# Neighbourhood attention with two heads on the array's halves, and routing tables stored in the layout of the tile

## The chip, the cores and the metric

One core of one Trainium2 chip runs the whole program. The time of a run is the device time of one execution in microseconds (us); lower is better. The kernel before took 2160.51 us (median of three runs, 2156.67 to 2163.53).

## The reference

Two transformer blocks in sequence over 512 tokens of width 1024. The first has a gated delta rule and a dilated window attention. The second mixes the tokens in three ways (4 heads of HGRN, 4 of RWKV7, 8 of neighbourhood attention over a grid of 8 rows by 64 columns), projects the mix with `w_out`, and ends in a mixture of experts (32 experts, two per token). The change is in the neighbourhood attention and in the tables of the router:

```python
def one_row(r):                       # all 8 rows share one window here
    s_win = einsum('bhjqd,bhrjkd->bhjqrk', q_row, k_blk) * scale     # 8 x 32 keys near a block of 16 columns
    s_win = where(in_win, s_win + rpb[...], NEG_INF)
    s_ctx = einsum('bhjqd,bhld->bhjql', q_row, kc_h) * scale         # 256 context keys, no bias
    prob  = softmax(concatenate([s_win, s_ctx], -1))
    return einsum(p_win, v_blk) + einsum(p_ctx, vc_h)
```

So each of 8 heads has four column blocks j; a head and block has 128 queries (8 rows x 16 columns), 256 window keys, 256 context keys, and head size 64.

## The kernel before, in words

The kernel is written in tiles; a scheduler places each engine's instructions by priority and by readiness, and an engine then runs its list in order. What stands where on an engine is therefore a result of the whole program.

**Neighbourhood attention** is the generator `na()` (kept in `self.heads`; one `next` issues one unit). A pair p of heads (p = 0 to 3) lies on the 128 partitions of q and k, head b on half b of them. `prepare(p)` loads and rotates q and k and loads the values `nvw` (window) and `nvt` (context) and the bias `nb`. There are 32 units (p, j, b):
- `scores`: two matmuls of 64 rows by 256 columns (L1630 window, L1631 context) into one PSUM bank `ns`; on DVE the bias and the maximum (L1633), the maximum of the context half (L1635) and the negated larger one (L1636); on ACT two exponentials of 256 columns that also sum (L1637, L1638).
- `turned`: four 128x128 transposes (L1644) into the bank `nT` and a copy to SBUF, by DVE for b = 1 (L1647), by ACT for b = 0 (L1649).
- `values`: four matmuls (L1658) with the turned probabilities as the stationary 128x128 operand and 64 value columns moving, into a quarter of the bank `no`. After the eighth of a pair the result is divided by the sums (L1663 to L1666) and `put_one` turns it back (L1678) and splits it into the high and low parts `mxh` and `mxl` (L1681, L1682).

**Around it.** The first unit is prepared at the start of `hgrn()` and `na_beside` issues one unit between the steps of HGRN; all others follow in the loop of `run()`, which at unit `na_at` also issues `out_start()` and the output projection of k = 0 and 1. The output projection of k multiplies one 128-row slice of the mix, as high and low parts, by `w_out`: for each of 8 column blocks m three fp32r matmuls of 512 columns (L312 to L314, `mm3`) per k into a PSUM bank `g` (three banks in the pool `gp`), then one DVE instruction that adds the block to x (L1789). The weights `wo` come through SP's DMA queue, ACT makes the high part (L297), POOL the low (L298). k = 4 to 7 use the four pairs of the attention. Then come `tail`, `route` and `experts`.

**The tables.** `route` stores the index and weight tables of the lots beyond the first 32 into DRAM (`ovi`, L2032; `ovw`, L2035), from tiles with the slot on the partition to tables with the lot first, so an element of 8 or 4 bytes at a time. SP issues these stores and then `eod` and the expert weights `er` (1 MB each, L2101). Only the loop of `more_experts` reads the tables, and it runs no times on these inputs.

Of the kernel before, what the change touches and what calls it, by code (L numbers as in the profile page):

```python
# [10 lines left out]
F32 = mybir.dt.float32  # L11
# [7 lines left out]
P = 128  # L19
# [175 lines left out]
def na_bias(rpb):  # L195

    q, k = np.arange(P), np.arange(256)
# [8 lines left out]
    return np.ascontiguousarray(np.stack(out, 2))  # L206
# [64 lines left out]
class Kern:  # L271
# [1282 lines left out]
    def na(self):  # L1554
# [20 lines left out]
        def prepare(p):  # L1575
# [31 lines left out]
            bias = nw.tile([P, 2, 3, 256], F32, tag="nb", name=self.name("nb"), bufs=2)  # L1607
            nc.sync.dma_start(bias, I["b_na"][2 * p:2 * p + 2].rearrange("b p k x -> p b k x"))
# [9 lines left out]
        def scores(p, j, b):  # L1618

            nonlocal ready  # L1620
            if j + b == 0:
                work[p] = (*ready, nw.tile([P, 4, 2, 3], F32, tag="nst", name=self.name("nst"), bufs=2))
                if p < 3:
                    ready = prepare(p + 1)
            q, k, vt, vw, bias, st = work[p]
            r, s = half[b], lambda i: st[:, j, b, i:i + 1]
# [5 lines left out]
            pr = nw.tile([P, T], F32, tag="np", name=self.name("np"), bufs=4)  # L1632
            nc.vector.tensor_tensor_reduce(out=pr[:, :256], in0=ps[:, :256], in1=bias[:, b, (0, 1, 1, 2)[j], :],  # L1633
                                           scale=1.0, scalar=NEG, op0=OP.add, op1=OP.max, accum_out=s(0))
            nc.vector.tensor_reduce(s(1), ps[:, 256:], AX.X, OP.max)  # L1635
            nc.vector.tensor_scalar(s(2), s(0), s(1), -1.0, OP.max, OP.mult)  # L1636
            nc.scalar.activation(pr[:, :256], pr[:, :256], AF.Exp, bias=s(2), accum_out=s(0))  # L1637
            nc.scalar.activation(pr[:, 256:], ps[:, 256:], AF.Exp, bias=s(2), accum_out=s(1))  # L1638
            return pr

        def turned(b, pr):
            pt = psum("nT", self.nt)
            for x in range(4):
                nc.tensor.transpose(pt[:, x * P:(x + 1) * P], pr[:, x * P:(x + 1) * P], ident)  # L1644
            pT = nw.tile([P, T], F32, tag="nT", name=self.name("npT"), bufs=3)
            if b:
                nc.vector.tensor_copy(pT, pt)  # L1647
            else:
                nc.scalar.activation(pT, pt, AF.Copy)  # L1649
            return pT  # L1650

        def values(p, j, b, pT):
            q, k, vt, vw, bias, st = work[p]
            if j + b == 0:
                self.po = psum("no", 1).rearrange("p (j b d) -> p j b d", j=4, b=2)
            hv = half[b]
            for x, v in enumerate((vw[:, j, 0, hv], vw[:, j, 1, hv], vt[:, 0, hv], vt[:, 1, hv])):
                nc.tensor.matmul(self.po[:, j, b, :], pT[:, x * P:(x + 1) * P], v, start=x == 0, stop=x == 3)  # L1658
            if (j, b) != (3, 1):
                return  # L1660

            den = nw.tile([P, 4, 2], F32, tag="nden", name=self.name("nden"), bufs=2)
            nc.vector.tensor_add(den, st[:, :, :, 0], st[:, :, :, 1])  # L1663
            nc.vector.reciprocal(den, den)
            on = nw.tile([P, 4, P], F32, tag="no", name=self.name("non"), bufs=2)
# [665 lines left out]
```

## Time and profile before

| | before |
|---|---|
| device time, median of three runs | 2160.51 us (2156.67 to 2163.53) |
| the profiled execution: time | 2169.63 us |
| the profiled execution: span | 2167.8 us |
| busy: PE, weight loads, DVE, ACT, POOL | 88%, 63%, 45%, 31%, 27% |
| mean granted TensorE clock | 0.882 |

The profile is of one execution, 9.1 us longer than the median of the runs. The engines are PE (matmul), PEld (weight load), DVE, ACT, POOL and SP, which issues most DMAs; the granted clock (PEclk) is a share of 2.4 GHz, so that 0.50 is 1.2 GHz. The shares above are means over stages that are bound by different things; the rows below are therefore taken from the stages that the change touches. An fp32 matmul leaves two records in the trace, an fp32r matmul or a transpose one.

### The profile page before, as it was taken

Reading aid. Unit: us, or ns where it says so; the run is one execution under the profiler, and the core shown is the slowest. Engines: PE = TensorE matmul, PEld = TensorE weight load, DVE = VectorE, ACT = ScalarE, POOL = GpSimd, SP = SyncE. Lnnn points to the kernel's source line nnn. Section 1 sums busy time; section 2 is a strip of 40 time slices with the busy share of each in tenths; the row PEclk is TensorE's granted clock in tenths of the full one; section 3 lists DMA queues with packets and bytes.
Section 4 is the critical chain, followed back from the end, with each engine's and each line's share of the span. In section 5 each row is a group of like instructions: output and inputs, shape, how many; then the busy total and the mean of one; then the engine's idle time right before and its main releaser. Section 6 shows DMA issues by size and latency. Waiting matters only on the chain.

```text
span 2167.8 us, 30545 instructions
## 1 busy us (share of the span) xinstructions
PE 1907.4 (88%) x11925; PEld 1359.7 (63%) x11925; DVE 969.1 (45%) x2095; ACT 682.4 (31%) x1306; POOL 581.6 (27%) x407
## 2 busy tenths in 40 slices
PE   6988898998999998999989995598996999999886
PEld 4665575676667777766788774476785555444442
DVE  5434742775761146157565545754356322222110
ACT  6652336444623244433322235342222101000000
POOL 3224322344375553412111115611001010101011
PEclk9878899999989999978887896676578999999999
DMA  3111232456622252222121227233046999999997
GB/s 127 40 49 46 66 100 87 156 175 203 195 83 93 95 186 96 77 62 68 48 69 42 71 93 239 84 100 91 13 175 263 228 412 417 413 416 412 415 413 280
DMA packets 137215, 363.18 MB, mean 168 GB/s; under 512 B 47950, under 2 KB 67566, under 8 KB 112366
## 3 DMA queue, kind: packets, MB, share of 16 engines
q1 hardware_dynamic: 126558, 340.34, 43.1%
q10 hardware_dynamic: 5472, 15.05, 2.8%
q0 software_dynamic: 5040, 5.82, 1.4%
q8 instruction: 95, 1.56, 0.3%
q14 instruction: 50, 0.41, 0.1%
HBM read 332.49 MB, written 26.55 MB: 166 GB/s over the span
## 4 chain that ended last, share of the span: by engine, by line
PE 36%; DMA 15%; issue 10%; DVE 7%; POOL 4%; ACT 3%; SPq 0%; POOLq 0%; ACTq 0%; DVEq 0%
DMA out_dram<-ey,sidx 12%; PE g L314 6%; PE g L312 6%; PE g L313 6%; PE no L1658 2%; POOL lo L298 2%; PE gu L2129 2%; PE nT L1644 1%; DVE stmp L624 1%; PE ns L1631 1%; DVE sX L625 1%; PE ns L1630 1%; PE rm L1116 1%; DMA wo<-in_w_o_dram 1%; PE tr L2065 1%
## 5 line engine op out<-in xcount | busy, mean ns | idle before, releaser
L298 POOL TENSOR_TENSOR lo<-wraw,hi 128x1024 fp32r<-128x1024 f32 (+1 forms) x127 | 298.4, 2351 | 582.2 <-ACT hi L297 510.9
L312 PE MATMUL g<-h1hi,hi 128*128 128x512 f32 (+1 forms) x584 | 253.1, 433 | 11.7 <-ACT gt L439 7.5
L2129 PE MATMUL gu<-er,xw 128*64 128x256 f32 x2048 | 240.6, 383 | 20.2 <-DMA er<-in_w_e_dram 18.7
L314 PE MATMUL g<-h1hi,lo 128*128 128x512 f32 (+1 forms) x584 | 249.8, 428 | 6.4 <-POOL lo L298 6.4
L313 PE MATMUL g<-h1lo,hi 128*128 128x512 f32 (+1 forms) x584 | 252.4, 432 | 3.1 <-DVE h1lo L355 1.6
L297 ACT ACTIVATE hi<-wraw 128x1024 fp32r<-128x1024 f32 (+1 forms) x127 | 127.4, 1004 | 315.7 <-PE g L313 161.2
L2129 PEld LDWEIGHTS gu<-er,xw 128*64 128x64 f32 x2048 | 143.9, 137 | 112.6 <-DMA er<-in_w_e_dram 27.4
L2158 POOL DMA_INDIRECT out_dram<-ey,sidx x32 | 50.4, 1574 | 466.2 <-DVE ey L2157 365.9
L312 PEld LDWEIGHTS g<-h1hi,hi 128*128 128x128 f32 (+1 forms) x584 | 118.0, 202 | 46.6 <-ACT gt L439 8.4
L314 PEld LDWEIGHTS g<-h1hi,lo 128*128 128x128 f32 (+1 forms) x584 | 117.3, 201 | 44.0 <-POOL lo L298 11.2
L313 PEld LDWEIGHTS g<-h1lo,hi 128*128 128x128 f32 (+1 forms) x584 | 117.9, 202 | 38.1 <-issue 8.3
L2154 PE MATMUL py<-er,es 128*64 128x512 f32 x512 | 121.0, 604 | 1.8 <-SPq L2200 1.0
L2132 ACT ACTIVATE eg<-gu 128x256 f32<-128x256 f32 x32 | 12.2, 383 | 249.6 <-PE gu L2129 249.6
L312 PE MATMUL g<-hlhi,hi 128*128 128x512 f32 x200 | 85.5, 427 | 5.0 <-ACT hlhi L949 4.6
L313 PE MATMUL g<-hllo,hi 128*128 128x512 f32 x200 | 85.6, 428 | 0.0
L2065 PE MATMUL tr<-h,S 128*128 128x512 f32 x256 | 74.7, 422 | 12.3 <-DVE xw L2074 7.1
L314 PE MATMUL g<-hlhi,lo 128*128 128x512 f32 x200 | 85.4, 427 | 0.0
L2157 DVE SCALAR_TENSOR_TENSOR ey<-py,wslot,g2row 128x512 f32<-128x512 f32 x32 | 24.0, 751 | 127.9 <-PE py L2154 113.9
L2154 PEld LDWEIGHTS py<-er,es 128*64 128x64 f32 x512 | 34.1, 137 | 61.7 <-issue 54.7
L2133 DVE TENSOR_TENSOR eh<-eg,gu 128x256 f32<-128x256 f32 x32 | 13.3, 417 | 129.1 <-ACT eg L2132 129.1
L2065 PEld LDWEIGHTS tr<-h,S 128*128 128x128 f32 x256 | 45.8, 195 | 39.7 <-issue 20.5
L896 DVE CUSTOM_DVE_ANT_0 aw<-aw,acc 128x1024 f32<-128x1024 f32 x48 | 66.8, 1397 | 7.8 <-DMA aw<-in_w_ada_dram 7.4
(658 smaller groups left out, 3848.6 us busy)
## 6 DMA issues: line engine op xcount, KB each, us to landing
er<-in_w_e_dram SPq DMA_DIRECT2D x192, 1024.0 KB
aw<-in_w_ada_dram SPq DMA_DIRECT2D x48, 512.0 KB
wraw<-in_w_qkv_dram SPq DMA_DIRECT2D x36, 512.0 KB
wraw<-in_w_g_dram SPq DMA_DIRECT2D x12, 512.0 KB
dxs<-draw SPq DMA_DIRECT2D x96, 64.0 KB
wraw<-in_w_rw_dram SPq DMA_DIRECT2D x9, 512.0 KB
wraw<-in_w_ga_dram SPq DMA_DIRECT2D x8, 512.0 KB
wraw<-in_w_gb_dram SPq DMA_DIRECT2D x8, 512.0 KB
```

Of the source, the lines that this page charges most:

```text
L297: nc.scalar.activation(hi, raw, AF.Copy)
L298: (lo_engine or nc.gpsimd).tensor_sub(lo, raw, hi.bitcast(F32))
L312: nc.tensor.matmul(ps, lh, rh, start=start, stop=False, **kw)
L313: nc.tensor.matmul(ps, lh, rl, start=False, stop=False, **kw)
L314: nc.tensor.matmul(ps, ll, rh, start=False, stop=stop, **kw)
L896: nc.vector.tensor_tensor_reduce(out=w, in0=w, in1=cc, scale=1.0, scalar=0.0, op0=OP.mult, op1=OP.add, accum_out=self.modl[:, m:m + 1])
L1658: nc.tensor.matmul(self.po[:, j, b, :], pT[:, x * P:(x + 1) * P], v, start=x == 0, stop=x == 3)
L2065: nc.tensor.matmul(ps[:n], S[:, i, :n], self.h2[i][a][:, c], start=i + a == 0, stop=i + a == 4)
L2129: nc.tensor.matmul(ps[64 * c:64 * c + 64, a, :], xs(2 * i + k), w[:, k, a, c, :], start=i + k + a == 0, stop=i == 3 and k == 1 and a == 1, ...
L2154: nc.tensor.matmul(py[64 * c:64 * c + 64], hs[:, k, 64 * i:64 * i + 64], part[:, k, c, :], start=i + k == 0, stop=i + k == 2)
L2157: nc.vector.scalar_tensor_tensor(y, py, w, self.g2, OP.mult, OP.mult)
L2158: nc.gpsimd.indirect_dma_start(out=self.O["out_0"].rearrange("t (h d) -> (t h) d", h=2), out_offset=bass.IndirectOffsetOnAxis(ap=idx, axis ...
```

## The change

Scores, exponentials and values are written for a pair of heads at a time, 16 units (p, j):
- The four score matmuls alternate between the two row halves of the array (head 0 on rows 0 to 63, head 1 on rows 64 to 127), each head into its own PSUM bank.
- The bias tile is 7 slots of 256 with a slot of zeros in the middle; a strided slice picks the bias of the block and the zeros, so that one DVE instruction of 512 columns does bias and maximum, and one exponential of 512 columns follows per head.
- In `values` the value tile (64 columns) is now stationary and the turned probabilities move (128 columns); the heads alternate between the two column halves of the array, and the result lies with the head dimension on the partitions. It needs no turning back. The division multiplies by 1/sum spread over the partitions, by a wide copy and four matmuls with the identity.
- PSUM: `gp` falls from three banks to one, `nsp` holds two score banks and one for transposes; for k = 4 to 7 most blocks m of the projection take a score bank. `na_at` goes from 2 to 1.
- The tables are stored with the slot first, as the tiles hold them.

```diff
-            ps = psum("ns", 2) if self.nth % 3 or self.mixed is None else self.nsp.tile([P, T], F32, tag="ns", name=self.name("ns"))
+            if self.nth % 2 or self.mixed is None:
+                ps = [psum("ns", 2) for _ in range(2)]
+            else:
+                ps = [self.nsp.tile([P, T], F32, tag="ns", name=self.name("ns"), bufs=2) for _ in range(2)]
...
-            nc.tensor.matmul(ps[:, 0:256], q[r, j, :], kg[r, :, KS[j]:KS[j] + 32], start=True, stop=True)
-            nc.tensor.matmul(ps[:, 256:512], q[r, j, :], k[r, 0:TC], start=True, stop=True)
...
+            for b, r in enumerate(half):
+                nc.tensor.matmul(ps[b][:, 0:256], q[r, j, :], kg[r, :, KS[j]:KS[j] + 32], start=True, stop=True)
+            for b, r in enumerate(half):
+                nc.tensor.matmul(ps[b][:, 256:512], q[r, j, :], k[r, 0:TC], start=True, stop=True)
...
+                nc.vector.tensor_tensor_reduce(out=two(pr[b]), in0=two(ps[b]), in1=bias[:, at[b], :], scale=1.0,
+                                               scalar=NEG, op0=OP.add, op1=OP.max, accum_out=st[:, j, b, 0:1])
+            nc.vector.tensor_scalar(st[:, j, :, 1], st[:, j, :, 0], -1.0, None, OP.mult)
+            for b in range(2):
+                nc.scalar.activation(pr[b], pr[b], AF.Exp, bias=st[:, j, b, 1:2], accum_out=st[:, j, b, 0:1])
...
-            for x, v in enumerate((vw[:, j, 0, hv], vw[:, j, 1, hv], vt[:, 0, hv], vt[:, 1, hv])):
-                nc.tensor.matmul(self.po[:, j, b, :], pT[:, x * P:(x + 1) * P], v, start=x == 0, stop=x == 3)
+            for x, v in enumerate((vw[:, j, 0], vw[:, j, 1], vt[:, 0], vt[:, 1])):
+                for b, r in enumerate(half):
+                    nc.tensor.matmul(self.po[r, j * P:(j + 1) * P], v[:, r], pT[b][:, x * P:(x + 1) * P],
+                                     start=x == 0, stop=x == 3)
...
+            nc.vector.reciprocal(den, st[:, :, :, 0])
+            wide = nw.tile([P, 4, 2, 64], F32, tag="no", name=self.name("nwd"), bufs=1)
+            nc.vector.tensor_copy(wide, den[:, :, :, None].to_broadcast([P, 4, 2, 64]))
+            pb = psum("nT", 1)
+            for i in range(4):
+                nc.tensor.matmul(pb[:, i * P:(i + 1) * P], wide[:, i].rearrange("p b d -> p (b d)"), ident, start=True, stop=True)
...
+            nc.scalar.activation(on, pb, AF.Copy)
+            nc.vector.tensor_mul(on, on, self.po)
...
-            ps = self.gp.tile([P, T], F32, tag="g", name=self.name("g"))
+            if a < 4 or m % 3 == 0:
+                ps = self.gp.tile([P, T], F32, tag="g", name=self.name("g"))
+            else:
+                ps = self.nsp.tile([P, T], F32, tag="ns", name=self.name("g"), bufs=2)
...
-        self.ovi = self.dp.tile([16, P, 2], I32, name="ovi")
-        self.ovw = self.dp.tile([16, P], F32, name="ovw")
+        self.ovi = self.dp.tile([P, 16, 2], I32, name="ovi")
+        self.ovw = self.dp.tile([P, 16], F32, name="ovw")
...
-        nc.sync.dma_start(self.ovi.rearrange("c s a -> s c a"), ov)
+        nc.sync.dma_start(self.ovi, ov)
...
-        self.na_at = 2
+        self.na_at = 1
...
-                pool(e4, "gp", 3, space=PSUM, side="right")
+                pool(e4, "gp", 1, space=PSUM, side="right")
```

**The order of the instructions.** Before the attention all engines' lists are alike; from there on PE, DVE, ACT and SP differ (PE has 5768 rows in place of 5704, DVE 2023 in place of 2072). On PE, in the middle of the attention, the list before reads (`ns` are scores, `nT` transposes, `no` values; 64-wide moving operands):

```order
L1630 MATMUL ns_11853<-nk_11631,nq_11621 128x256
L1644 MATMUL nT_11767<-c_10448,np_11761 128x128 x4
L1658 MATMUL no_11693<-nvw_11345,npT_11752 128x64 x2
L1658 MATMUL no_11693<-nvt_11343,npT_11752 128x64 x2
L1631 MATMUL ns_11853<-nk_11631,nq_11621 128x256
L1644 MATMUL nT_11787<-c_10448,np_11781 128x128 x4
L1658 MATMUL no_11693<-nvw_11345,npT_11772 128x64 x2
```

and with the change, where a unit stands whole (scores of two heads into two banks, transposes, then values with `v` stationary):

```order
L1637 MATMUL ns_11896<-nk_11607,nq_11597 128x256
L1637 MATMUL ns_11897<-nk_11607,nq_11597 128x256
L1639 MATMUL ns_11896<-nk_11607,nq_11597 128x256
L1639 MATMUL ns_11897<-nk_11607,nq_11597 128x256
L1655 MATMUL nT_11873<-c_10448,np_11866 128x128 x4
L1655 MATMUL nT_11880<-c_10448,np_11867 128x128 x4
L1670 MATMUL no_11887<-npT_11829,nvw_11614 64x128
L1670 MATMUL no_11887<-npT_11836,nvw_11614 64x128
L1670 MATMUL no_11887<-npT_11829,nvw_11614 64x128
L1670 MATMUL no_11887<-npT_11836,nvw_11614 64x128
```

The scores of two heads now stand side by side, and so do the values of two heads, whose two `npT` alternate. Most units are broken up by others, as at the next place.

At the first matmuls of the output projection (`g`), the list of PE before has all 48 of k = 0 and 1 in one bunch:

```order
L1630 MATMUL ns_11645<-nk_11338,nq_11328 128x256
L1631 MATMUL ns_11645<-nk_11338,nq_11328 128x256
L312 MATMUL g_11446<-mxh,woh_11436 128x512
L313 MATMUL g_11446<-mxl,woh_11436 128x512
L312 MATMUL g_11454<-mxh,woh_11436 128x512
L313 MATMUL g_11454<-mxl,woh_11436 128x512
L314 MATMUL g_11446<-mxh,wol_11437 128x512
```

With the change they stand in groups of six among the values and transposes of the attention, of which this is the second:

```order
L316 MATMUL g_11452<-mxh,wol_11449 128x512
L1655 MATMUL nT_11634<-c_10448,np_11627 128x128 x4
L1670 MATMUL no_11406<-npT_11576,nvw_10952 64x128
L1670 MATMUL no_11406<-npT_11569,nvt_10950 64x128
L1655 MATMUL nT_11641<-c_10448,np_11628 128x128 x2
L314 MATMUL g_11460<-mxh,woh_11442 128x512
L315 MATMUL g_11460<-mxl,woh_11442 128x512
L316 MATMUL g_11460<-mxh,wol_11443 128x512
L314 MATMUL g_11460<-mxh,woh_11448 128x512
L315 MATMUL g_11460<-mxl,woh_11448 128x512
L316 MATMUL g_11460<-mxh,wol_11449 128x512
L1655 MATMUL nT_11641<-c_10448,np_11628 128x128 x2
```

The groups of one bank `g` are apart by the attention's instructions, and the eight groups end about 90 rows after the first; behind them 118 rows of the attention alone follow, up to the projection of k = 4. Counted from the first of these to the last value matmul, PE's list before has 46 score matmuls, 104 transposes, 108 value matmuls, 16 transposes back and 68 matmuls of the projection, and changes 56 times between whole array, row halves and column halves; with the change it has 40, 100, 109, 16 (the spread of 1/sum) and 58, and changes 72 times. Of the value matmuls 86 stand directly behind one on the other column half, of the score matmuls 18 behind one on the other row half.

On SP, where the `wo` of k = 4 and on are loaded (`nkr` belongs to the preparation of the last pair, `nvw` and `nvt` are its values), the list before is

```order
L1588 DMA nt_11833<-nkc 128x256
L1589 DMA nt_11834<-nkr 128x1x768
L1781 DMA wo_12216<-in_w_o_dram 128x8x128
L1781 DMA wo_12262<-in_w_o_dram 128x8x128
L1781 DMA wo_12308<-in_w_o_dram 128x8x128
L1781 DMA wo_12354<-in_w_o_dram 128x8x128
L1610 DMA nvw_11638<-nvw 128x1x256
```

and with the change

```order
L1590 DMA nt_11791<-nkc 128x256
L1612 DMA nvw_11614<-nvw 128x1x256 x4
L1607 DMA nvt_11612<-nvd 128x2x128
L1591 DMA nt_11792<-nkr 128x1x768
L1793 DMA wo_12144<-in_w_o_dram 128x8x128
L1793 DMA wo_12190<-in_w_o_dram 128x8x128
L1793 DMA wo_12236<-in_w_o_dram 128x8x128
```

The four `nvw` and the `nvt`, whose buffers come free when an earlier pair's values are done, now stand ahead of the `wo` of k = 4 to 7.

## Rows read from the trace of the kernel before

**Rows 1.** The page, the chain that ended last, shares of the span by line.
```profile
DMA out_dram<-ey,sidx 12%; PE g L314 6%; PE g L312 6%; PE g L313 6%; PE no L1658 2%; POOL lo L298 2%; PE gu L2129 2%; PE nT L1644 1%; DVE stmp L624 1%; PE ns L1631 1%; DVE sX L625 1%; PE ns L1630 1%; PE rm L1116 1%; DMA wo<-in_w_o_dram 1%; PE tr L2065 1%
```

**Rows 2.** Windows: us, busy (instructions) of PE, PEld, DVE, ACT, POOL; PEclk, DMA share, GB/s.
```profile
1412.00:1439.00 27.00, 23.64 (x204) 18.74 (x200) 14.85 (x44) 13.67 (x23) 2.48 (x2) 1.00 0.24 79
1466.00:1480.00 14.00, 11.56 (x55) 9.25 (x53) 10.13 (x17) 0.00 (x0) 2.50 (x2) 0.98 0.47 127
1480.00:1596.00 116.00, 111.70 (x393) 85.30 (x394) 38.44 (x120) 33.62 (x109) 4.66 (x2) 0.50 0.09 28
1461.00:1600.00 139.00, 132.26 (x490) 101.97 (x489) 51.75 (x145) 35.79 (x117) 7.16 (x4) 0.56 0.15 43
```

**Rows 3.** Timeline of PE at half clock: start, duration, engine, line, operation, tiles, count.
```profile
1503.94 1.22 PE L1630 MATMUL ns<-nk,nq 64*128 64x256 f32 x2
1505.09 1.11 PE L1644 MATMUL nT<-c,np 128*128 128x128 f32 x4
1506.00 0.95 PE L1658 MATMUL no<-nvw,npT 128*128 128x64 f32 x4
...
1507.73 1.22 PE L1631 MATMUL ns<-nk,nq 64*128 64x256 f32 x2
```

**Rows 4.** Timeline of PE at full clock, two heads beside HGRN.
```profile
1430.07 0.66 PE L1644 MATMUL nT<-c,np 128*128 128x128 f32 x4
1430.56 0.56 PE L1658 MATMUL no<-nvw,npT 128*128 128x64 f32 x4
...
1431.50 0.70 PE L1630 MATMUL ns<-nk,nq 64*128 64x256 f32 x2
1432.03 0.59 PE L1631 MATMUL ns<-nk,nq 64*128 64x256 f32 x2
```

**Rows 5.** Timeline of PE: two of the bunch of projection matmuls, at full clock.
```profile
1468.33 0.40 PE L313 MATMUL g<-mxl,woh 128*128 128x512 f32 x1
1468.56 0.40 PE L314 MATMUL g<-mxh,wol 128*128 128x512 f32 x1
```

**Rows 6.** Timeline of PE: HGRN's matmuls that alternate row halves (L1449) and column halves (L1509).
```profile
1367.35 2.18 PE L1449 MATMUL hm<-ht,ht 64*128 64x128 f32 x32
...
1409.78 2.39 PE L1509 MATMUL hm<-hvt,hkt 128*64 128x64 f32 x40
```

**Rows 7.** Lines of DVE in 1480 to 1596: count, busy us, mean ns, idle before.
```profile
L1647 DVE COPY npT<-nT 128x512 f32<-128x512 f32 x12 | 8.3, 691 | 29.9 <-PE nT L1644 29.9
L1789 DVE SCALAR_TENSOR_TENSOR x1b<-g,modl,x1b 128x512 f32<-128x512 f32 x4 | 3.0, 751 | 4.0 <-PE g L314 4.0
```

**Rows 8.** Lines of ACT in 1480 to 1596.
```profile
L1649 ACT ACTIVATE npT<-nT 128x512 f32<-128x512 f32 x12 | 7.1, 595 | 44.8 <-PE nT L1644 44.8
L1638 ACT ACTIVATION_READ_ACCUMULATOR np<-ns,nst 128x1 f32 x23 | 4.5, 195 | 0.0
```

**Rows 9.** Lines of DVE in 1600 to 1660: a 512-column instruction that multiplies and sums.
```profile
L1820 DVE CUSTOM_DVE_ANT_1 nq<-x1b 128x512 f32<-128x512 f32 x5 | 3.2, 688 | 4.4 <-ACT x1b L1819 4.2
```

**Rows 10.** The chain in 1440 to 1520, in order of time: start, us, what.
```profile
1464.00 18.60 DMA wo<-in_w_o_dram
```

**Rows 11.** Timeline of SP's queue at the tables: issue, us to landing, line, transfer.
```profile
1684.90 0.83 SPq L2035 DMA_DIRECT2D ovw<-ows  x1
1685.83 5.70 SPq L2037 DMA_DIRECT2D eod<-eoi  x1
1693.10 18.93 SPq L2101 DMA_DIRECT2D er<-in_w_e_dram  x9
```

**Rows 12.** Windows behind the tables and the whole experts' stage, columns as in rows 2.
```profile
1686.00:1692.00 6.00, 3.43 (x10) 1.88 (x12) 3.85 (x9) 2.61 (x5) 0.00 (x0) 0.72 1.20 22
1704.00:1710.00 6.00, 6.00 (x46) 3.08 (x44) 2.90 (x5) 0.38 (x1) 2.12 (x1) 1.00 0.59 102
1710.00:1716.00 6.00, 6.00 (x48) 3.13 (x46) 0.42 (x1) 0.38 (x1) 0.00 (x0) 1.00 1.01 389
1708.00:2140.00 432.00, 391.70 (x2616) 205.71 (x2616) 87.92 (x149) 37.16 (x83) 45.12 (x29) 1.00 1.02 413
```

More of the change, by code (lines that the diff above doesn't have):

```diff
@@ L1606, in prepare @@
             vw = nw.tile([P, 4, 2, P], F32, tag="nvw", name=self.name("nvw"), bufs=2)
[L1607 to L1608 removed]
+            bias = nw.tile([P, 7, 256], F32, tag="nb", name=self.name("nb"), bufs=2)
+            nc.sync.dma_start(bias, I["b_na"][p])
             for j, k0 in enumerate(KS):
@@ L1616, in na, with scores @@
         work, done = {}, []
-        def scores(p, j, b):
+        def scores(p, j):
             nonlocal ready
-            if j + b == 0:
-                work[p] = (*ready, nw.tile([P, 4, 2, 3], F32, tag="nst", name=self.name("nst"), bufs=2))
+            if j == 0:
+                work[p] = (*ready, nw.tile([P, 4, 2, 2], F32, tag="nst", name=self.name("nst"), bufs=2))
                 if p < 3:
@@ new lines, in scores @@
+            for b, r in enumerate(half):
+                nc.tensor.matmul(ps[b][:, 256:512], q[r, j, :], k[r, 0:TC], start=True, stop=True)
+            two = lambda ap: ap.rearrange("p (a x) -> p a x", a=2)
+            pr = [nw.tile([P, T], F32, tag="np", name=self.name("np"), bufs=4) for _ in range(2)]
+            for b in range(2):
+                nc.vector.tensor_tensor_reduce(out=two(pr[b]), in0=two(ps[b]), in1=bias[:, at[b], :], scale=1.0,
+                                               scalar=NEG, op0=OP.add, op1=OP.max, accum_out=st[:, j, b, 0:1])
@@ new lines, in scores, with turned @@
+            nc.vector.tensor_scalar(st[:, j, :, 1], st[:, j, :, 0], -1.0, None, OP.mult)
+            for b in range(2):
+                nc.scalar.activation(pr[b], pr[b], AF.Exp, bias=st[:, j, b, 1:2], accum_out=st[:, j, b, 0:1])
+            return pr
+        def turned(pr):
+            pT = []
+            for b in range(2):
+                pt = psum("nT", 1) if b or self.mixed is None else self.nsp.tile([P, T], F32, tag="nT", name=self.name("nT"), bufs=1)
+                for x in range(4):
+                    nc.tensor.transpose(pt[:, x * P:(x + 1) * P], pr[b][:, x * P:(x + 1) * P], ident)
+                pT.append(nw.tile([P, T], F32, tag="nT", name=self.name("npT"), bufs=4))
+                if b:
+                    nc.vector.tensor_copy(pT[b], pt)
+                else:
+                    nc.scalar.activation(pT[b], pt, AF.Copy)
@@ L1684, in na @@
+                hi, lo = (gr(u[:, 2 + p, :]) for u in self.mixed)
+                on = on.rearrange("p (j r c) -> p j r c", j=4, c=16)
+                nc.scalar.activation(hi, on, AF.Copy)
+                nc.vector.tensor_sub(lo, on, hi.bitcast(F32))
         self.nth = 0
-        units = [(p, j, b) for p in range(4) for j in range(4) for b in range(2)]
+        units = [(p, j) for p in range(4) for j in range(4)]
         pr, pT = {}, {}
@@ L1691, in na @@
             if 0 <= t < len(units):
-                pT[t] = turned(units[t][2], pr.pop(t))
+                pT[t] = turned(pr.pop(t))
             if v >= 0:
@@ L2224, in run @@
         self.epss, self.wraw_bufs = {}, 2
-        self.nt, self.skew = 1, (0, 1)
+        self.skew = 0, 1
         def pool(es, name, bufs=1, **kw):
```

54 lines of the change are left out of this document (14 added, 40 removed).

## The prediction

> **What bounds the kernel now.** I read the chain of waits first: it gives the share of the span that sets the end, by line. The attention's matmuls (L1658, L1644, L1630, L1631) hold about 5% of it between them, and the experts' output transfers 12% [rows 1]. The reader should see two things: that the attention is on the path, and that the last stage is paced by transfers. The table of windows then says by what. From the first projection matmul to the attention's last values the core takes 139 us, in which PE is busy for 132, DVE for 52 and ACT for 36, at a mean clock of 0.56; the middle 116 us run at 0.50, that is at 1.2 GHz, with PE busy for 111.7 [rows 2]. So PE bounds this stretch, at the lower of its two levels, although it hardly ever stands. In the experts' stage the weights bound: 432 us at 413 GB/s, DMA share 1.02, with PE busy for 392 [rows 12]. What is gained before that stage, or in the first loads of it, comes off the end.
>
> **Prices on PE, from the timeline.** At half clock [rows 3] four transposes take 1505.09 to 1506.00, .91 us, or .23 each; a head's four value matmuls (eight records) take 1506.00 to 1507.73, 1.73, or .43 each; a score matmul between other work takes 1503.94 to 1505.09, 1.15. At full clock [rows 4] it is .49 for four transposes (.12 each), .94 for four values (.235), .53 for a score. A score matmul has 512 columns to stream in two records, and with twice the columns of a value record its own time is .43 (full) and .85 (half); the remainder of a visit, .10 and .30, is what the change of tiling costs around it. The values' end holds a further .09 or so. I take .14 for each change of tiling at full clock and .25 at half. A projection matmul costs .23 at full clock [rows 5], about .43 at half (scaled by the transposes' ratio).
>
> **Do neighbours on opposite halves run together?** HGRN shows both kinds. Thirty-two records on alternating row halves take 2.18 us at full clock, .068 each, where a transposes' record takes .12 [rows 6, 4]. Forty on alternating column halves take 2.39 us, .06 each, at half clock, where such a record takes .22 by itself [rows 6, 3]. Both are fp32, as in the change. So I give each matmul that stands directly behind one on the other half one record less: .11 for a value, .215 for a score, at full clock.
>
> **The sum for the stretch.** The counts are those of the order lists, first projection matmul to last values. As a test, before at half clock: 46 scores x .85 + 104 transposes x .23 + 108 values x .43 + 16 x .23 + 48 projections x .23 (these ran at full clock) + 20 x .43 + 56 changes x .25 = 147 us against 139 measured; 6% too much, of which a few us ran at full clock [rows 2]. After, at full clock: scores 40 x .43 - 18 x .215 = 13.3; values 109 x .22 - 86 x .11 = 14.5; transposes 100 x .12 = 12; the spread of 1/sum 16 x .22 = 3.5; projections 58 x .23 = 13.3; changes 72 x .14 = 10.1. That is 66.7 us. To it I add 4 for a beginning at half clock and 13 for waits, below: 84, so 55 less.
>
> **Waits that I add.** DVE has per pair two 512-column sums of .69 [rows 9] with .08 each for reading the sum, .21 for the negation, and one copy of .69 [rows 7]: 2.44 us, 12.5 pairs of them 31; with some ten additions to x at .75 [rows 7] and four divisions of about 2.3 (a copy, a product and a split at .69, a small one), 47 us. ACT has per pair two exponentials of about .6 with .195 each to read the sum, and a copy of .595 [rows 8]: 2.2, some 38 with splits. Both are under 67, so PE stays the bound, but they were a third of it and are now 70%, and each unit's chain scores, DVE, ACT, transposes, copy, values has one unit of skew to hide in. The `wo` weights of k = 4 take 18.6 us to land on the chain before [rows 10], behind other work; they now stand behind `nvw` and `nvt` on SP, which wait for an earlier pair's values, and ACT's split of them stands in ACT's list ahead of copies that transposes wait for. One bank `g` makes each group wait .75 for DVE, which the attention's own matmuls between the groups cover. I take 13 us for all of it, between 4 (only the tail of `wo`, as before) and 25 (the whole landing once, and the skew).
>
> **What the page on tiling says against it.** The rows show .14 to .25 us for a change of tiling [rows 3, 4], and there are 72 in place of 56. The Trainium skill, page "TensorEngine Tiling (Array Packing)", section Key Properties, says that changing the tiling mode, as opposed to the tile, drains the engine; the trace agrees so far as a change costs something, and by that rule each of the 16 further changes costs its price again, which the sum has. The same page, section PSUM Bottleneck, says that tiling makes TensorE faster but not the emptying of PSUM; it would make DVE the bound if the 47 us above were short.
>
> **After the stretch.** Ten projection matmuls more are left for the end: 10 x .23 = 2.3 us back. HGRN's stretch, where seven heads' transposes stand in place of six, may give 2. Beyond it, tail, router and experts keep their order.
>
> **The tables.** Stored element by element they are 2 x 2048 packets of 8 and 4 bytes. After their issue the windows show DMA engines busy (1.20, .59) with 22 and 102 GB/s, up to 1710; then 389 and on to 413 [rows 12]. `eod` takes 5.7 us behind them, and the `er` loads go out at 1693.1 and land 18.9 later [rows 11]. From there the stage is paced by the weights, so what the loads are late is late at the end. With 128 packets of 128 and 64 bytes I take the loads to flow from about 1695: 14 us. The bounds are 8 (the landing of the first piece was needed no earlier than that: PE stands only about 3 us in 1686 to 1692, the slack that the weights later have not got) and 23 (from 1687, at once behind the issue).
>
> **Sum.** 55 - 2 + 2 + 14 = 69 us. Against the profiled execution, 2169.6 - 69 = 2100.6; that execution lay 9.1 above the median, in no stage that I can name, so I take the same off the median: 2160.5 - 69 = **2092 us**.
>
> **The ways it can go.**
> - **A, full clock** (chance .50): as summed. The granted clock was 1.00 in 1412 to 1439, where units of the attention alternate with HGRN's column pairs, and .98 in the bunch of projections [rows 2]. Now the projections are spread over the first third of the stretch and neighbours on both halves keep more of the array at work. With waits and tables at their bounds, 2074 to 2105.
> - **B, the clock falls where the attention stands alone** (.27): behind the last of the 48 projections some 118 rows of PE's list are pure attention, about half of the attention's work. At half clock that part takes about 28 us more: 84 + 28 = 112, 27 less than before, with the tables 41: 2120, or 2110 to 2126. The trace speaks for it: 116 us of attention at .50 with PE busy [rows 2]. The Trainium skill, "TensorE: Matmul & The Clock Gate", Part 1, has the clock follow the engine's activity; no row here shows how much the pairs count for.
> - **C, half clock throughout** (.12): 13.3, 14.5, 12, 3.5 twice over (87), projections 58 x .43 = 25 or, in full-clock spells, 13, changes 72 x .25 = 18, less the 6% of the test: 111 to 122, with 4 of waits; 13 to 24 less, with the tables 2122 to 2134.
> - **D, slower: the neighbours do not overlap** (.06). fp32 matmuls of 64 and 128 partitions write one PSUM bank from both column halves; if they go one after the other, the clock has no reason to rise either. Then 40 x .85 + 109 x .43 + 23 + 7 + 25 + 18 = 154, with 5 of waits 159 against 139: 20 - 14 = 6 slower, 2167, and for each .1 us that a change of half costs, 104 x .1 = 10 more: 2167 to 2190. It decides from the point at which under a quarter of the 104 pairs run together at half clock. HGRN's rows [rows 6] speak against it.
> - **E, serial but at full clock**, or only the tables' gain (.05): 13 us above A's sum, 2105 to 2118, or some 2146 where only the tables gain.
>
> A is the likeliest. The range 2074 to 2134 takes in A, B, C and most of E; left out are D and what lies below A's bound. About 0.3% (6 us) is what a measurement of this kernel can tell from no change. Faster: A, B, C and E nearly whole, .92; within 0.3%, an edge of D and a C without tables, .03; slower, D and a wait that I don't see, .05.
>
> **What would show it.** Right: the stretch from first projection matmul to last values takes 80 to 90 us; PEclk is above .9 in most of its windows; eight pairs of value records take about .9 us at full clock (16 records in 1.8); the windows behind the tables show over 350 GB/s within 10 us of their issue. B shows as .50 in the pure part alone, C as .50 nearly throughout. Idle PE in front of transposes, released by ACT or DVE, for over 20 us in sum would show that I took the waits too small. I am wrong in the main if the value matmuls on opposite halves are spaced like single ones, .22 at full clock, or if the experts' stage ends no earlier although it starts earlier.

## The result and the profile after

The changed kernel takes **2091.28 us** (median of four runs, 2088.25 to 2096.92) against 2158.59 for the kernel before in the same rounds (2149.48 to 2163.53): ratio 0.9696, 95% interval 0.9657 to 0.9735, or 57 to 74 us less. Six later runs gave 2089.34 to 2098.23. The forecast was 2092. The number came out; the experiments show that the premise under its largest term, that single heads run at half clock, did not. Of the runs below one of `small`, at 2159.05 us, counts as a slow one and stands outside its ratio.

The profiled execution after took 2096.92 us (span 2094.9), at a mean granted clock of 0.906 in place of 0.882. First the windows that answer to [rows 2]: the stretch from the first projection matmul (1461.8) to the last values (1537), then behind the tables. Columns as there.

```profile
1462.00:1538.00 76.00, 69.65 (x487) 47.54 (x487) 49.37 (x101) 31.54 (x70) 11.31 (x6) 0.96 0.27 81
1626.00:1632.00 6.00, 3.67 (x11) 2.07 (x13) 3.62 (x9) 2.40 (x5) 0.00 (x0) 0.74 0.12 38
1632.00:1638.00 6.00, 6.00 (x42) 3.80 (x40) 0.75 (x1) 0.38 (x1) 1.48 (x1) 0.98 0.60 220
1638.00:1644.00 6.00, 6.00 (x49) 3.35 (x47) 1.47 (x3) 0.38 (x1) 0.22 (x1) 1.00 1.00 347
```
The stretch is 75 us in place of 138, at a mean PEclk of .96 in place of .56. DVE's busy time is nearly what it was (49 of 76 us, before 52 of 139), PE's is 70 in place of 132. The tables' stores leave at 1624.2; 38 GB/s flow while the next weights still wait for a buffer, 220 in the next six microseconds, and full speed from about 1638. The end comes 470.7 us after the first store, before 483.4.

The timeline of PE, answering to [rows 3, 4], at full clock:

```profile
1445.89 0.70 PE L1637 MATMUL ns<-nk,nq 64*128 64x256 f32 x4
1446.42 0.60 PE L1639 MATMUL ns<-nk,nq 64*128 64x256 f32 x4
...
1457.78 0.66 PE L1670 MATMUL no<-npT,nvw 128*64 128x128 f32 x8
1458.27 0.60 PE L1670 MATMUL no<-npT,nvt 128*64 128x128 f32 x8
1458.81 0.70 PE L1637 MATMUL ns<-nk,nq 64*128 64x256 f32 x4
```
Four records of score matmuls for two heads (L1637) take .53 us, as long as two for one head took before; eight records of value matmuls, for two heads in turn, take .49 where a head's eight took .94 [rows 4]. So neighbours on opposite halves do run together. What PE waited for in the stretch, in all, times, longest:

```profile
PE nT L1655 <- ACT np L1647: 3.7, 4, 2.7
PE g L314 <- DVE x1b L1804: 1.5, 2, 1.3
PE no L1670 <- DVE npT L1658: 1.0, 1, 1.0
```
That is 6.2 us, in seven pieces. In the kernel before PE stood once in this stretch, for longer, in front of a transpose; this is its timeline of PE, then of ACT:

```profile
1475.07 0.60 PE L1644 MATMUL nT<-c,np 128*128 128x128 f32 x4
...
1476.97 0.59 PE L1631 MATMUL ns<-nk,nq 64*128 64x256 f32 x2
1484.30 1.11 PE L1644 MATMUL nT<-c,np 128*128 128x128 f32 x4 [6.74 <-ACT npT L1649]
```
```profile
1481.09 1.06 ACT L297 ACTIVATE woh<-wo 128x1024 fp32r<-128x1024 f32 x1 [17.26 <-DMA wo<-in_w_o_dram]
1482.71 1.06 ACT L297 ACTIVATE woh<-wo 128x1024 fp32r<-128x1024 f32 x1 [0.56 <-DMA wo<-in_w_o_dram]
1483.67 0.58 ACT L1649 ACTIVATE npT<-nT 128x512 f32<-128x512 f32 x1
```
ACT's list had the split of the projection's weights (L297) ahead of the copy `npT` (L1649); ACT stood 17.26 us for the weights' landing, and PE stood 6.74 behind the copy. Four transposes show .60 up to there and 1.11 from there on, and the clock stayed at .50 up to 1596 [rows 2]. After the change ACT stands only a little in that place:

```profile
1489.58 1.06 ACT L299 ACTIVATE woh<-wo 128x1024 fp32r<-128x1024 f32 x1 [2.21 <-DMA wo<-in_w_o_dram]
```
Yet PE still stood 2.66 us, up to 1494.5, and the clock fell there too. It came back after about 7 us, with no projection matmul in between (the eight groups of k = 0 and 1 had ended at 1488.7), and stayed:

```profile
1496.00:1502.00 6.00, 5.50 (x22) 3.13 (x23) 3.80 (x13) 2.12 (x5) 0.00 (x0) 0.50 0.85 281
1504.00:1537.00 33.00, 32.34 (x257) 22.28 (x256) 19.57 (x51) 16.72 (x39) 0.00 (x0) 1.00 0.07 21
```
A second execution of the same kernel (`changed_again`, below) stood 4.69 us in one piece, and its clock went the same way, again without a projection in between:

```profile
PE nT L1655 <- ACT np L1647: 5.2, 3, 4.7
1490.00:1496.00 6.00, 5.78 (x20) 3.44 (x20) 3.38 (x11) 2.88 (x9) 0.00 (x0) 0.50 0.60 195
1497.00:1532.00 35.00, 34.34 (x275) 23.67 (x273) 20.55 (x52) 16.74 (x40) 0.00 (x0) 1.00 0.06 20
```
To compare executions whose earlier, unchanged parts differ by some microseconds, I read two marks in each: HGRN's first product on ACT (`ht`, L1430, after L1432) and SP's first load of expert weights (`er`, L2101, after L2116), which waits for the end of the attention. Their rows before, then after:

```profile
1331.46 0.72 ACT L1430 ACTIVATE ht<-ht 128x256 f32<-128x256 f32 x2
```
```profile
1601.82 3.19 SPq L2101 DMA_DIRECT2D er<-in_w_e_dram  x6
```
```profile
1339.02 0.72 ACT L1432 ACTIVATE ht<-ht 128x256 f32<-128x256 f32 x2
```
```profile
1542.13 3.10 SPq L2116 DMA_DIRECT2D er<-in_w_e_dram  x6
```
270.4 us before, 203.1 after: 67 less. Of these 7 lie ahead of the stretch (130.0 us before, 122.8 after), 63 in it, and 3 are lost behind it. From the second mark to the end of the span: 566.0 and 552.8, 13 less. The execution after was 7.6 us later at the first mark, in code that is the same; so 67 + 13 - 8 = 72 is what the two spans differ by (72.9).

### The profile page after: what moved, and what is told of

Same layout as the page of the kernel before. It is cut to its first block, busy times and chain, and to the rows that moved or that the text cites. A ratio compares the mean times of both kernels' runs of the same rounds, so it can differ in the third digit from the quotient of the medians.

```text
span 2094.9 us, 30479 instructions
## 1 busy us (share of the span) xinstructions
PE 1841.7 (88%) x11941; PEld 1304.6 (62%) x11941; DVE 970.0 (46%) x2047; ACT 676.9 (32%) x1246; POOL 579.8 (28%) x407
## 4 chain that ended last, share of the span: by engine, by line
PE 32%; DMA 16%; issue 11%; DVE 7%; ACT 4%; POOL 4%; SPq 0%; POOLq 0%; ACTq 0%; DVEq 0%
DMA out_dram<-ey,sidx 13%; PE g L316 6%; PE g L314 6%; PE g L315 6%; DVE sX L627 1%; PE rm L1118 1%; POOL lo L300 1%; DVE stmp L626 1%; PE rm L1068 1%; PE gu L2144 1%; ACT hi L299 1%; DMA wor<-in_w_o_dram 1%; PE tr L2080 1%; DMA nt<-nqk 1%; PE no L1670 1%
```

## The experiments

All are compared with the kernel before in the same rounds. "Stage" is the time between the two marks, "stretch" from the first projection matmul to the last values, "rest" from the second mark to the end, all of the profiled execution.

| kernel | median, us | ratio (95%) | stage | stretch | rest |
|---|---|---|---|---|---|
| before | 2158.6 to 2165.0 in four sets | | 270.4 | 138.4 | 566.0 |
| changed | 2091.28 | .9696 (.9657 to .9735) | 203.1 | 75.1 | 552.8 |
| changed again | 2094.17 | .9674 (.9647 to .9700) | 202.3 | 73.9 | 553.3 |
| tables | 2154.59 | .9951 (.9933 to .9969) | 267.9 | 137.5 | 552.6 |
| attention | 2105.68 | .9723 (.9683 to .9762) | 204.5 | 75.2 | 563.8 |
| values_serial | 2092.95 | .9662 (.9623 to .9700) | 207.3 | 76.1 | 553.2 |
| values_as_before | 2097.52 | .9685 (.9646 to .9724) | 208.0 | 83.2 | 556.2 |
| heads_apart | 2114.27 | .9795 (.9750 to .9841) | 212.7 | 85.8 | 553.9 |
| split_on_pool | 2108.80 | .9735 (.9687 to .9783) | 212.1 | 81.4 | 562.7 |
| small | 2104.49 | .9729 (.9700 to .9759) | 212.4 | 81.7 | 553.5 |
| skew12 | 2093.35 | .9660 (.9609 to .9711) | 204.1 | 68.1 | 555.5 |
| na_at2 | 2098.60 | .9700 (.9651 to .9748) | 206.2 | 74.3 | 553.3 |
| both_on_pool | 2092.23 | .9655 (.9627 to .9683) | 202.1 | 73.5 | 553.9 |
| prep_on_pool | 2088.60 | .9643 (.9613 to .9672) | 201.2 | 70.2 | 554.5 |

**The two parts apart.** `tables` is the kernel before with the tables alone:

```diff
-        self.ovi = self.dp.tile([16, P, 2], I32, name="ovi")
+        self.ovi = self.dp.tile([P, 16, 2], I32, name="ovi")
...
-        nc.sync.dma_start(self.ovi.rearrange("c s a -> s c a"), ov)
+        nc.sync.dma_start(self.ovi, ov)
```

> The kernel before with only the two tables stored slot first. In the trace of the changed kernel the way from the first table store to the end of the span takes 470.7 us, before it took 483.4. Theory (the weights' stream starts late behind the small packets, and what it is late is late at the end): 12.7 us less than before, about 2146, and the windows behind the tables over 350 GB/s within 10 us after the next weight load is issued. Rival (the stores are only late themselves, the stream has slack later): under 4 us less.

`attention` is the changed kernel with these lines undone.

> The changed kernel with the tables stored as before. Theory (the two parts are independent and add up): 67 - 13 = 54 us less than before, about 2104, with the 20-odd GB/s behind the tables back. Rival (the attention's gain is what the tables' gain needs, or the other way round): more than 5 us away from that sum.

The tables alone gain 11 us (7 to 15 by the interval), the attention alone comes to 2105.7, within 2 of the sum. The rests agree: 566.0, 562.7 and 563.8 with the old tables, 552.6 to 556.2 with the new ones. The parts add up, and the tables are worth 9 to 13 us.

**The pairs of values.** `values_serial` exchanges two loops of the changed kernel:

```diff
-            for x, v in enumerate((vw[:, j, 0], vw[:, j, 1], vt[:, 0], vt[:, 1])):
-                for b, r in enumerate(half):
+            for b, r in enumerate(half):
+                for x, v in enumerate((vw[:, j, 0], vw[:, j, 1], vt[:, 0], vt[:, 1])):
```

> The changed kernel with the two loops of the value matmuls exchanged, so that the four matmuls of one head stand together and then the four of the other: in PE's list 12 of 108 value matmuls stand behind one on the other column half, in place of 86 of 109. Nothing else is edited. Theory 1, only the overlap is lost and the clock stays at full: 74 x .11 = 8 us more than the changed kernel, about 2099. Theory 2, the pairs also hold the clock up: the stretch from the first projection matmul to the last values shows PEclk near .5 for a good part, and the time is 30 to 45 us over the changed kernel, 2121 to 2136. Rival, the gain comes from the 128 moving columns and from fewer DVE and ACT instructions: under 4 us more, at full clock.

Windows of the stretch, and PE's waits there:

```profile
1456.00:1533.00 77.00, 73.65 (x482) 52.84 (x482) 43.90 (x100) 30.92 (x69) 8.16 (x5) 0.98 0.23 69
```
```profile
PE nT L1655 <- ACT np L1647: 3.1, 2, 2.7
1492.00:1495.00 3.00, 3.00 (x13) 2.34 (x14) 0.69 (x1) 1.13 (x4) 0.00 (x0) 0.50 0.52 132
```
The mean clock stayed near full (.98): it fell behind a stand of 2.75 us and was back 3.4 us later. The time is that of the changed kernel (2092.95). So the value pairs do not hold the clock; theory 2 falls. Nor do they give the 8 us of theory 1: PE is busy 4.0 us more, it stands 3.0 us less (77.0 - 73.65 against 76.0 - 69.65), and the stretch is 1 to 2 us longer, the stage 4 to 5. Where PE is the bound by so little, what it saves comes back in part as waiting.

`values_as_before` goes further and puts the values back as they were, with the transposes back:

```diff
-                    nc.tensor.matmul(self.po[r, j * P:(j + 1) * P], v[:, r], pT[b][:, x * P:(x + 1) * P],
+                    nc.tensor.matmul(self.po[:, j, b, :], pT[b][:, x * P:(x + 1) * P], v, start=x == 0, stop=x == 3)
```

> The changed kernel with the values as they were: probabilities stationary, 64 value columns moving, whole array, and the four transposes back; scores, bias, exponentials, PSUM pools and tables stay as changed. Theory 1 (overlap of values alone): 108 value matmuls at .22 in place of 14.5 us, 9 us more than the changed kernel, about 2100, at full clock. Theory 2 (the values' column halves hold the clock up): PEclk near .5 in the stretch and 35 to 50 us more, 2126 to 2141. Rival (scores and softmax bring the gain): within 4 us of the changed kernel.

```profile
1484.00:1494.00 10.00, 9.88 (x61) 7.51 (x61) 5.58 (x9) 4.10 (x7) 3.88 (x2) 1.00 0.11 28
1498.00:1514.00 16.00, 16.00 (x68) 13.34 (x67) 5.72 (x14) 4.04 (x11) 0.00 (x0) 0.50 0.23 68
1516.00:1540.00 24.00, 24.00 (x172) 19.33 (x172) 12.39 (x34) 10.40 (x25) 0.00 (x0) 1.00 0.00 1
```
2097.5, 6 over the changed kernel and between the 9 of theory 1 and the 4 of the rival, with overlapping intervals; the stretch is 8 us longer. The windows show how the clock moves: full up to a stand of 2.35 us at 1494 (PE waited for an exponential), .50 behind it, and full again from 1515, with PE busy in every microsecond of both. What PE ran just ahead of the rise are eight records of scores on alternating halves and eight transposes.

**One head at a time, and the stand alone.** `heads_apart` is the changed kernel, written for single heads:

```diff
-            for b in range(2):
-                nc.scalar.activation(pr[b], pr[b], AF.Exp, bias=st[:, j, b, 1:2], accum_out=st[:, j, b, 0:1])
-            return pr
+                nc.scalar.activation(pr, pr, AF.Exp, bias=st[:, j, b, 1:2], accum_out=st[:, j, b, 0:1])
+                yield pr
...
+            for b in range(2):
+                if both is not None:
+                    pT[i, b] = turned(b, next(both))
+                if i:
+                    values(*units[i - 1], b, pT.pop((i - 1, b)))
```

> The changed kernel with one head at a time: scores, one 512-column bias and maximum, one exponential, transposes and values of head 0, then of head 1 (one more negation per unit). Column halves, order of the division, PSUM pools, na_at and tables stay as changed. In PE's list 6 of 96 value matmuls and 9 of 42 scores stand behind one on the other half, in place of 86 and 18. The two earlier runs without value pairs kept the clock at full, and both fell to half after PE stood over 2 us and rose again where score pairs run. Theory A (the score pairs lift the clock again): without them PEclk stays near .50 from the first stand on to the late projections, and the time is 30 to 45 us over the changed kernel, 2121 to 2136. Theory B (the clock at full is lost by a long stand alone; the changed kernel has short ones): PEclk mostly over .8 and 8 to 15 us more, from the overlap lost, 2099 to 2106. Theory C (the overlap and the pairs are nothing): under 4 us more.

```profile
1460.00:1470.00 10.00, 0.73 (x2) 0.64 (x3) 3.71 (x5) 0.75 (x2) 2.48 (x2) 0.58 0.34 109
1470.00:1480.00 10.00, 10.00 (x47) 7.20 (x46) 5.24 (x13) 2.00 (x5) 0.00 (x0) 0.74 0.31 83
1480.00:1536.00 56.00, 55.34 (x360) 38.98 (x360) 31.01 (x85) 24.67 (x54) 4.69 (x2) 1.00 0.15 48
```
The median is 23 us over the changed kernel, between the ranges of theories B and A, but the runs are 2096.45 to 2124.55, and the profiled one is the fastest. In it PE stood 10.3 us at 1459 (a projection matmul waited for DVE's addition to x, which stood behind the landing of an input of a later pair), the clock fell, came back behind six projection matmuls and a unit's values, and stayed at 1.00 for the remaining 56 us of single heads, PE busy for 55, from 1486 to 1531 without a projection matmul. In this execution single heads kept the full clock, as in theory B. What the slower runs lost is in no trace.

`split_on_pool` is the kernel before, with one edit that takes the copy out from behind the landing:

```diff
-            wc.append(self.split(raw, 0, *(op.tile([P, KD, P], F32R, tag="wo" + u, name=self.name("wo" + u), bufs=2)
-                                           for u in "hl")))
+            hi, lo = (op.tile([P, KD, P], F32R, tag="wo" + u, name=self.name("wo" + u), bufs=2) for u in "hl")
+            if a < 4:
+                self.split(raw, 0, hi, lo)
+            else:
+                nc.gpsimd.tensor_copy(hi, raw)
+                nc.gpsimd.tensor_sub(lo, raw, hi.bitcast(F32))
+            wc.append((hi, lo))
```

> The kernel before, where the high part of the projection's weights of k = 4 to 7 is made on POOL in place of ACT, so that no exponential stands in ACT's list behind the landing of these weights; all else as before, single heads and the bunch of 48 projections too. PE's 6.7 us of waiting at 1478 to 1484 should go. Theory B (the half clock of the attention comes from that stand, and PE keeps the level it has while it is busy): the stretch runs at full clock, 50 to 60 us less than before, about 2100 to 2110. Theory A (single heads cannot hold or regain the full clock, the pairs do): 4 to 8 us less, PEclk .50 within 15 us of the end of the bunch. Between: the level falls at another, later stand, and the gain is in proportion.

Its windows, first the bunch of projections, then the attention of single heads; and ACT's first copy behind the bunch:

```profile
1466.00:1476.00 10.00, 10.00 (x51) 8.29 (x49) 7.13 (x12) 0.56 (x1) 1.98 (x2) 1.00 0.42 118
1476.00:1540.00 64.00, 63.92 (x407) 49.06 (x406) 41.04 (x127) 31.58 (x108) 7.25 (x5) 1.00 0.21 61
```
```profile
1475.44 0.60 ACT L1649 ACTIVATE npT<-nT 128x512 f32<-128x512 f32 x1 [11.32 <-PE nT L1644]
```
This decides where the half clock before came from. ACT copies at 1475.4, 8 us sooner than before, PE does not stand, and the same single-head attention runs for 64 us at 1.00 with PE busy for 63.92. PE's order is not quite that of before: the scheduler drew one group of projections forward to 1485.6, so that the longest stretch without one is 17 us in place of 62. That projections hold the level is unlikely, since in `heads_apart` it lasted 44 us without one. In all fourteen traces each fall within the stretch stands behind a wait of PE, of 1.3 to 10.3 us, and in the three without a wait over 1.5 us (`split_on_pool`, `small`, `prep_on_pool`) it never fell. The stretch is 81.4 us in place of 138.4, the kernel 2108.8 in place of 2163.5. Of the stage's 67 us, 58 (270.4 - 212.1; 56 against the 267.9 of `tables`) are had without any pair of heads.

`small` adds the tables to that edit, on the kernel before.

> The kernel before with two edits only: the tables stored slot first, and the high part of the projection's weights of k = 4 to 7 made on POOL. No pairs, no other softmax, no other PSUM pools. By the two single runs, 55 and 11 us less than before, it should come to about 2097 to 2100. Theory B (the attention's half clock came from one stand of PE): that sum holds, the stretch of the attention is at full clock, and of the changed kernel's gain all but 4 to 10 us is had without a pair of heads. Rival (the two do not add, or the single heads lose the clock again in some runs): over 2106, or a spread of more than 20 us over the runs.

The stage repeats (212.4; PE busy for 83.00 of 83 us at .97), and so does the rest (553.5). The ratio, .9729, is 12 us short of the changed kernel's in the same rounds (.9674), 4 to 7 us worse than I expected of the sum and over the 4 to 10 of theory B; its stage is 10 longer. The profiled run is the fastest, 2089.34, and the others in the ratio are 2102.86 to 2112.09. So the rival's sign, a spread of more than 20 us, came too; that single heads lose the clock in some runs is not excluded, since only the fastest was traced.

**Order and waits of the changed kernel.** Four runs sought what is left. `skew12` is `self.skew = 1, 2`, `na_at2` is `self.na_at = 2`.

> The changed kernel with transposes one unit and values two units behind the scores (skew 1, 2 in place of 0, 1): the chain scores, DVE, ACT, transposes has a unit more to hide in. In the changed kernel PE stands about 8 us in all between 1442 and 1540, most of it for ACT's exponentials. Theory (these waits are hidden by a longer skew): 4 to 8 us less than the changed kernel, about 2085. Rival (DVE's preparation of the next pair is what is late, the skew moves the wait elsewhere): within 3 us.

> The changed kernel with the first output projection issued after the second unit of the loop, as before, in place of the first. Theory (the order of the first projections matters little): within 3 us of the changed kernel, 2088 to 2094. Rival (the earlier start of the projections filled the stands of the first units): 4 us or more slower.

`skew12` shortens the stretch to 68.1 us, but it starts later, and the stage is the same (204.1): the wait moved. The median is the changed kernel's, within a spread of 26 us. `na_at2` is 3 us longer in the stage and 7 in the median, with overlapping intervals: not settled.

`both_on_pool` gives the changed kernel the edit of `split_on_pool`; `prep_on_pool` also this:

```diff
-                nc.vector.tensor_mul(raw[:, L], raw[:, L], tab[:, a, 0])
-                nc.vector.tensor_add(raw[:, L], raw[:, L], xs)
+                (nc.gpsimd if p else nc.vector).tensor_mul(raw[:, L], raw[:, L], tab[:, a, 0])
+                (nc.gpsimd if p else nc.vector).tensor_add(raw[:, L], raw[:, L], xs)
```

> The changed kernel with the high part of the weights of k = 4 to 7 made on POOL in place of ACT. PE's order is the same row for row. Theory (ACT's four splits of 1.06 us and their wait for the landing delay exponentials): 2 to 8 us less than the changed kernel in the same rounds. Rival (the change had already moved these splits out of the way): within 2 us.

> As the run before, and the first product and the sum of the rotation of q and k, two DVE instructions of .68 us each for both, are made on POOL for the pairs 1 to 3. The changed kernel's longest stand of PE (2.66 us at 1492, where the clock fell for about 10 us) ended with an exponential behind DVE's preparation of the last pair. Theory (that stand goes, the clock stays at full): 4 to 12 us less than the changed kernel. Rival (POOL takes 1.27 us for such an instruction, q and k come later and the stand is longer): no gain, or up to 10 us more.

> The changed kernel once more, for a second profile and for comparison within the same rounds. All theories: 2085 to 2097; the stretch from HGRN's last store to the experts' first weights about 100 us, as in the first profile (99.8), whatever the part of the program ahead of it takes.

The first edit gives the changed kernel nothing in the stage (202.1 against 202.3): ACT's wait for the weights was already short, and PE's longest stand remains (3.1 us). Run again, the changed kernel takes 101.0 us from HGRN's last store to the experts' first weights. In `prep_on_pool` that stand is gone, as its theory said: the longest is 1.4 us, and the clock is full over the whole stretch.

```profile
1457.00:1527.00 70.00, 67.93 (x483) 46.28 (x484) 42.04 (x96) 30.01 (x70) 14.15 (x9) 1.00 0.23 72
```
Its stage is the shortest of all, by 1 us, and its median the lowest, 2088.60 against 2094.17; 5.6 us is at the limit of what is told from no change, and the intervals overlap.

## Why the prediction was right, and where its reason was wrong

- **The stretch.** Forecast 84 us (66.7 of PE at full clock, 4 of a start at half, 13 of waits); measured 75.1 and 73.9, with PE busy for 69. The counts and the prices at full clock held: .53 for a pair of scores, .49 for eight records of values. The terms added for waits were too large: PE waited 6 and 5 us in place of 13, and in place of the start at half clock there were 7 us at half behind a stand. By the same prices the counts of before come to 19.8 + 12.5 + 23.8 + 1.9 + 15.6 + 7.8 = 81 us at full clock; `split_on_pool` took 81.4.
- **The clock, the step that failed.** Case A gave two reasons for the full clock: the projections are spread, and "neighbours on both halves keep more of the array at work". B, C and D rested on the 116 us of attention at .50 as a property of that work. It was none: nearly the same work ran at 1.00 in `split_on_pool`. The level had been lost in one stand of PE, which I had in view only as 4 us of waiting, "only the tail of `wo`, as before". Its price was the half clock of all that followed, some 55 us. With the units rewritten the scheduler placed ACT's split and the projections otherwise, and ACT stood 2.21 us where it had stood 17.26; I had read that move, and put it on the side of the costs. But the shorter wait is only part of the gain. In both traces of the changed kernel the level fell all the same, and came back after some 7 us. Had it stayed at half, the 35 us from 1502.6 to the last values would have taken up to 35 us more (an estimate, by twice the time). The spread projections did not bring it back, since none ran in between; whether the pairs did, as A would have it, is not shown. That A's time came is therefore in part luck.
- **What the rewritten attention is worth at full clock.** With single heads 212, with the change 202 to 203: 10 us of the stage, near the 14 that my own counts give (81 less 66.7). That is all its parts together; the value pairs alone show 1 to 2 in the stretch and 4 to 5 in the stage (`values_serial`). Serial heads at half clock, rival D, did not come, since two heads do overlap.
- **The tables.** Forecast 14 (8 to 23), measured 9 to 13. The mechanism was right. I had the weights flow from about 1695, that is 10 us after the store; in the trace they wait 8 us for a buffer and reach full speed 14 us after it, so the sign that I had named, 350 GB/s within 10 us, did not come.
- **The sum.** 55 + 14 - 2 + 2 = 69 was forecast. The traces show 67 + 13 = 80, with 63 in the stretch in place of 55, 7 ahead of it in place of 2, and 3 lost behind it. Of the 80, 8 are lost ahead of the first mark in that pair of executions; that mark came between 1321 and 1343 us in the fourteen traces. The medians differ by 67. The execution of before that I profiled was on the long side (stage 270.4, in `tables` 267.9). Some 10 us of the 80 are not found in the medians, and that 2092 and 2091 agree so closely is luck. One bound was added up wrong: with waits of 25 and tables of 8, case A comes to 2110, not 2105.
- **The pages.** The Trainium skill ("TensorEngine Tiling (Array Packing)", Key Properties) says that changing the tiling mode drains the engine. In the timeline after it cost little: the eight value records ahead of a score take .54 where the eight ahead of them take .49, less than the .14 that I had taken. The same page, section PSUM Bottleneck, says that emptying PSUM may become the bottleneck. It did not here: PE waited 2.5 us directly for DVE. On the clock the Trainium skill ("TensorE: Matmul & The Clock Gate", Why this matters for your kernels) asks for no gaps of PE between bursts of matmuls. The runs agree, with falls behind stands of 6.74 us before, 2.66 after and 10.3 in `heads_apart`, and that sentence would have named the cause.

What stays open: what brings the level back. In the kernel before it rose at about 1466.5, behind projection matmuls, and in `heads_apart` behind projections and a unit's values. In `values_as_before` it rose after 17 us, behind scores on alternating halves and transposes; in the changed kernel after some 7 us, behind its mixed units without a projection. In `values_serial` it rose after 3.4 us in which PE ran nothing but values, one head's matmuls after the other's on column halves, and transposes. It did not rise in 112 us of the kernel before, whose single heads move 64 value columns. So neither a projection nor a pair is needed, and "rose again where score pairs run" in the expectation for `heads_apart` does not fit `values_serial`. No run varies one of these alone at the same place.

## What to carry to other kernels

Where a long stretch runs at half clock with PE busy, look first at what PE did just before it fell: a single wait of a few microseconds may have cost the whole stretch, and taking that wait away can be worth more than a faster inner loop. When a rewrite of the inner loop gains, undo its parts one by one, and also try the smallest edit that removes the old wait; here one instruction moved to another engine gave 55 us, where the whole change gave 67. The tables stored a few bytes at a time held up the loads queued behind them, for 9 to 13 us at the end; store them as they lie.

## What was not expected of the hardware

A busy PE did not win the clock back. In the kernel before PE was busy for 111.7 of 116 us and stayed at .50 [rows 2]; nearly the same list of instructions, begun at full clock, kept 1.00 for 64 us in `split_on_pool`. In these two runs either level lasted under the same kind of work.

And two DVE instructions took many times their usual time while POOL ran two subtractions. The timelines of DVE and of POOL in the changed kernel:

```profile
1484.44 0.15 DVE L1645 TENSOR_SCALAR nst<-nst 128x2 f32<-128x2 f32 x1
...
1491.26 2.31 DVE L1645 TENSOR_SCALAR nst<-nst 128x2 f32<-128x2 f32 x1
1493.49 2.66 DVE L1595 SCALAR_TENSOR_TENSOR nk<-nt,ngain,nt 128x256 f32<-128x256 f32 x1
```
```profile
1490.71 5.15 POOL L300 TENSOR_TENSOR wol<-wo,woh 128x1024 fp32r<-128x1024 f32 x2 [8.62 <-ACT woh L299]
```
L1645 takes .15 us at 1484.4 and 2.31 here; each of the two ends .3 us after one of POOL's two instructions of 2.6 us. That is where the longest wait of PE after the change, 2.7 us, came from: the exponentials stood behind L1645. In `changed_again` it was L1604 (2.73 us in place of .69) and L1645 (2.30), and the wait was 4.7. In `prep_on_pool` POOL's two instructions had ended before L1645, which took .15, and the longest wait was 1.4. The Trainium skill, page "SBUF — State Buffer", section "Who interferes with whom", has DVE and GpSimd share a pair of ports, which one of them can hold for a whole instruction while the other is blocked. The traces agree: L1645 took 2.31 us beside POOL and .15 without it.
